# A hybrid long-convolution and attention step: the first modulation block issued from ScalarE's queue, and the filter network's first layer finished later

## The chip, the cores and the metric

The kernel runs on one core of a Trainium2 chip. The metric is the device time of one execution in microseconds; the kernel before is told by the median of three runs. The core's engines each run their own instructions in order: TensorE (PE in the profile; its weight loads are PEld), VectorE (DVE), ScalarE (ACT), GpSimd (POOL) and SyncE (SP), which issues most DMAs. ScalarE can issue DMAs too, on a queue of its own. An engine waits for another one, or for a DMA, on semaphores.

## The reference, cut to what matters

Two groups of tokens (128 prompt rows and 512 sample rows, 1024 channels each) go through one layer with shared weights. What the change touches is the beginning: a modulation made from a conditioning vector, the first projections of the modulated rows, and a small network that makes the filters of the long convolution.

```python
def modulation(cond, w_ada, b_ada):
    mod = jax.nn.silu(cond) @ w_ada + b_ada
    return jnp.split(mod, 3, axis=-1)

def hyena_filters(L, f_w1, f_b1, f_w2, f_b2, f_w3, f_freq):
    ...
    z = jnp.concatenate([t, jnp.cos(bands * w), -jnp.sin(bands * w)], axis=-1)
    hf = jnp.sin(f_freq[0] * (z @ f_w1 + f_b1))
    hf = jnp.sin(f_freq[1] * (hf @ f_w2 + f_b2))
    hf = (hf @ f_w3).astype(jnp.float32).reshape(L, 2, D_HYENA)
    ...

def layer_forward(x, cond, ctx_kv, p):
    shift, scale, gate = modulation(cond, p["w_ada"], p["b_ada"])
    h = x * (1 + scale) + shift
    (v_h, x1, x0, g_h), (q, k, v, g_a), m = split_projection(h, p["w_in"], p["conv_w"], p["conv_b"])
    ...                                   # filters, long convolution, attention
    out = merge_branches(y_h, g_h, y_a.reshape(g_a.shape), g_a, m, p["w_bh"], p["w_ba"], p["w_out"])
    x_new = layer_norm(ALPHA * x + gate * out, p["ln_g"], p["ln_b"])
    return x_new, kv_out
```

## The kernel before, in words

All 640 rows stand side by side as columns, and the 1024 channels are cut into eight blocks of 128 (`k` = 0 to 7). Every large product is made with operands split into a high and a low part (`hH` and `hL` for the modulated rows, `wh` and `wl`, or `wf` and `wg`, for weights) and three matmuls instead of one.

The change lies in `prologue()` (L267), which runs over the eight channel blocks. For each block:

- two loads of 512 KB bring the block's columns of `w_ada`, one for the shift (part 0) and one for the scale (part 1), into the two halves of a tile `ada{k}`; three buffers take turns (tags `X`, `dftL`, `F`). `ada()` (L257) issues the load and then the 16 small matmuls into `adaT` (`psa` in the code);
- one load of 512 KB (`xw`) brings the block's rows of x and the weights of three projections for that block; three buffers take turns (tag `raw`);
- ScalarE copies `adaT` to `row`, TensorE turns it into columns (`modT`, L341), VectorE adds the bias (`mod`, L346); then VectorE and ScalarE make `hx`, `hH`, `hL` and the split weights `wf`, `wg` (L328 to L357);
- TensorE adds the block's share to three projections (L177, 18 matmuls of 128x320 a block). This is done one block late: `script` says that the products of block 0 are made while the modulation of block 1 is worked out, and so on. Entries such as `"00"` and `"80 10"` are projections 0, 8 and 1 with block 0; entries such as `"w3"` are matmuls on zeros (L281) that compute nothing the output needs and only keep TensorE busy in block 0.

Beside this loop runs the filter network (`hidden_layers()`, L244, a generator). Each of its two layers (`sin_layer()`, L222) is a product on TensorE into `ps_f` (L228), eight short VectorE instructions that reduce the argument of a sine (L230 to L239, the first of them one for each half in the second layer), and a Sine on ScalarE (L241). `step(n)` runs the generator over `n` yields: `step(7)` at block 0 and then the pairs in `layers`, whose first number is run in the middle of a block and whose second one at its end. So `step` and `layers` decide where the network's instructions stand among those of the blocks. In the kernel before, the second layer's product follows at the end of block 0.

The order on each engine is that of the code, as far as a scheduler of the toolchain doesn't put independent instructions the other way round; DMAs issued through `load_to` (L63) keep their order on SP. Eight semaphores for DMAs take turns, so a ninth DMA waits for the landing of the first. At the start SP issues a small pack with the conditioning vectors (`pack0`, 17 KB), the filter network's inputs (`zemb`, 82.5 KB) and its weights (`pack1`, 98 KB), and then the loads of block 0. The pack is needed by ScalarE for the gate of the conditioning vector (L297) and so by the modulation's matmuls; the other two by the network's first product.

After the prologue come the long convolution, the attention and the merge, in which the projections (L177) and a grouped product (L1182) take most of TensorE's time. The change leaves the order of instructions on every engine as it was from block 5 on.

Of the kernel before, what the change touches and what calls it, by code (L numbers as in the profile page):

```python
# [9 lines left out]
F32 = mybir.dt.float32  # L10
# [36 lines left out]
def tile_hyena_natten_step(ctx: ExitStack, tc: tile.TileContext, a, o):  # L47
    nc = tc.nc
    P = 128

    def f(ap):
        return ap.bitcast(F32)
# [10 lines left out]
    def load_to(dst, src):  # L63
        ins = nc.sync.dma_start(dst, src)
        last[:] = [ins]
        if pinned[0]:
            tc.keep_in_program_order(ins)
# [33 lines left out]
    def aux(name):  # L101
        return ps_ax.tile([P, 512], F32, tag="aux", name=name)
# [9 lines left out]
    def row(pool, tag, name, dt=F32, bufs=NK + 1):  # L112
        return pool.tile([P, NT], dt, tag=tag, bufs=bufs, name=name)
# [5 lines left out]
    def load_pack(i):  # L119
        pack = const.tile([P, sum(n for _, n in PACKS[i])], F32, tag=f"pack{i}", name=f"pack{i}")  # L120
        load_to(pack[:], a[f"pack{i}"])
        c0 = 0
        for name, n in PACKS[i]:
            out[name] = pack[:, c0 : c0 + n]
            c0 += n
# [43 lines left out]
    def bank(i, ps_pair=None):  # L169
        return ps_pair or [acc(f"mm{i}_{hf}") for hf in range(2)]  # L170

    def accumulate(ps, w, k, xh, xl, lead=(0, 1, 2)):
        passes = (w[0], xh), (w[0], xl), (w[1], xh)
        for i in lead:
            wt, x = passes[i]
            for hf in range(2):
                nc.tensor.matmul(  # L177
                    ps[hf][:, :HALF], wt[k], x[:, hf * HALF : (hf + 1) * HALF],
                    start=(i == 0 and k == 0), stop=(i == lead[2] and k == NK - 1), skip_group_check=True,
                )  # L180
# [27 lines left out]
    hw = hy.enter_context(tc.tile_pool(name="hw", bufs=1, side="right"))  # L208
# [3 lines left out]
    def temp(tag, name, bufs=1):  # L212
        return hw.tile([P, NT], F32, tag=tag, bufs=bufs, name=name)
# [41 lines left out]
    nc.gpsimd.memset(st[:], 0.0)  # L255

    def ada(ch, ps, raw):  # L257
        load_to(raw, a["wada"][ch])
        for t in range(2):
            for j in range(4):  # L260
                kt = 4 * t + j
                nc.tensor.matmul(  # L262
                    ps[32 * j : 32 * j + 32, :], st[:, kt, :], raw[:, P * kt : P * kt + P],
                    start=(t == 0), stop=(t == 1), skip_group_check=True, tile_position=(0, 32 * j),
                )

    def prologue():  # L267
        script = (
            ("w3", "w1", "w3", "w4"), ("", "", "00", "80 10"), ("", "", "01", "81 11"), ("", "", "02", "82 12"),
            ("", "", "03", "83 13"), ("", "", "04", "84 14"), ("", "", "05", "85 15"), ("", "", "06", "86 16 07 87 17"),  # L270
        )
        layers = ((1, 1), (0, 2), (0, 2), (0, 2), (1, 1), (0, 0), (0, 0), (0, 0))
        nc.vector.memset(f(hid[:, :256]), 0.0)
        front = (0, 8, 1)
        parts = {}

        def work(items):
            for item in items.split():
                if item[0] == "w":
                    for _ in range(int(item[1:])):  # L280
                        nc.tensor.matmul(banks[0][0][:, :256], hid[:, :P], hid[:, :256], start=True, stop=True, skip_group_check=True)  # L281
                else:
                    i, j = int(item[0]), int(item[1])
                    c = P * front.index(i)
                    accumulate(banks[i], [{j: t[:, c : c + P]} for t in parts[j]], j, hH[:, j], hL[:, j], lead=(0, 2, 1))

        def step(n):
            for _ in range(n):
                next(filt, None)

        out["zemb"] = temp("u", "zemb", 4)[:33]
        load_to(out["zemb"], a["zemb"])
        load_pack(1)
        th0 = const.tile([P, 2 * NK], F32, tag="th0", name="th0")
        spare = const.tile([P, 1], F32, tag="spare", name="spare")
        nc.gpsimd.memset(spare[:], 0.0)
        nc.scalar.activation(th0[:], cc, AF.Tanh, scale=0.5)  # L297
        nc.scalar.activation(spare[:], spare[:], AF.Sin)
        nc.vector.scalar_tensor_tensor(th0[:], th0[:], 1.0, cc, op0=ALU.add, op1=ALU.mult)
        nc.vector.tensor_scalar_mul(st[:, :, 0:2], th0[:].rearrange("p (k c) -> p k c", c=2), 0.5)  # L300
        nc.vector.tensor_copy(bss[:, 0], out["bss"][:, :NK])
        nc.vector.tensor_scalar_add(bss[:, 1], out["bss"][:, NK:], 1.0)
        for i in front:
            banks[i] = bank(i, (aux("mm1lo"), aux("mm1hi")) if i == 1 else None)
        filt = hidden_layers()
        for k in range(NK):
            xw = wp.tile([P, 1024], F32, tag="raw", bufs=3, name=f"xw{k}")
            psa = aux(f"adaT{k}")
            if k == 0:
                work("w12")  # L310
                step(7)
            pool, tag = ((hw, "X"), (hyc, "dftL"), (hw, "F"))[k % 3]
            wt = pool.tile([P, 2048], F32, tag=tag, name=f"ada{k}")
            for part in range(2):
                work(script[k][part])
                ada(part * 8 + k, psa[:, part * P : part * P + P], wt[:, 1024 * part : 1024 * part + 1024])
            row_ = hwa.tile([P, 2 * P], F32, tag="fb", bufs=3, name=f"row{k}")
            nc.scalar.activation(row_[:], psa[:, : 2 * P], AF.Copy)
            load_to(xw[:], a["xw"][k])
            xt, wf = xw[:, :NT], xw[:, NT:]  # L320
            wh = row(yhp, "yh", f"wf{k}", F32R)[:, : 3 * P]
            wl = row(yhp, "yh", f"wg{k}", F32R)[:, : 3 * P]
            parts[k] = wh, wl
            step(layers[k][0])
            if k >= 6:
                split(wh, wl, wf)
            else:
                nc.scalar.activation(wh, wf, AF.Copy)  # L328
            if k == 7:
                wraw(9)  # L330
                load_pack(2)
                out["convw"] = out["convw"].rearrange("p (i c) -> p i c", c=4)
                wraw(2)
                load_filter(0)
                out["dft"] = hw.tile([P, 2560], F32, tag="F", name="draw")
                load_to(out["dft"][:, :1280], a["dft"][:, :1280])
                w9 = hw.tile([P, 2, 1024], F32R, tag="X", name="w9")
            psm = aux(f"modT{k}")
            work(script[k][2])
            for c in range(2):  # L340
                nc.tensor.matmul(  # L341
                    psm[:, c * 2 : c * 2 + 2], row_[:, c * P : c * P + P], sel,
                    start=True, stop=True, skip_group_check=True,
                )
            mod = const.tile([P, 2, 2], F32, tag="mod", bufs=4, name=f"mod{k}")
            nc.vector.tensor_tensor(  # L346
                mod[:], psm[:, 0:4].rearrange("p (s c) -> p s c", s=2),
                bss[:, :, k : k + 1].to_broadcast([P, 2, 2]), op=ALU.add,
            )
            hx = hwa.tile([P, NT], F32, tag="cv", bufs=2, name=f"hx{k}")  # L350
            for c, s0, n in ((0, PC, LP), (1, SC, LS)):
                cs = slice(s0, s0 + n)
                nc.vector.tensor_scalar(hx[:, cs], xt[:, cs], mod[:, 1, c : c + 1], mod[:, 0, c : c + 1], op0=ALU.mult, op1=ALU.add)
                nc.scalar.activation(hH[:, k, cs], xt[:, cs], AF.Identity, scale=mod[:, 1, c : c + 1], bias=mod[:, 0, c : c + 1])
            if k < 6:
                nc.vector.tensor_tensor(wl, wf, f(wh), op=ALU.subtract)
            nc.vector.tensor_tensor(hL[:, k], hx[:], f(hH[:, k]), op=ALU.subtract)  # L357
            if k == 7:
                raw = raws.pop(9)
                nc.scalar.activation(w9[:, 0], raw[:], AF.Copy)  # L360
                low = nc.vector.tensor_tensor(w9[:, 1], raw[:], f(w9[:, 0]), op=ALU.subtract)
                early[2] = wtile(2)
                early[9] = [[w9[:, i, c : c + P] for c in range(0, 1024, P)] for i in range(2)]
            work(script[k][3])
            step(layers[k][1])
        now(filt)
        last.append(low)
# [1343 lines left out]
```

## Time and profile before

| | |
|---|---|
| median of 3 runs | 863.28 us (860.81 to 864.22) |
| profiled execution | 860.83 us, span 859.1 us |
| PE busy | 849.4 us, 99% of the span |
| DVE, ACT, POOL busy | 678.7, 464.7, 131.4 us |
| DMA | 138.64 MB, mean 161 GB/s |
| DMA in the first 43 us (two slices of 40) | 352 and 359 GB/s |

The profile is a record of one execution. Its span runs from the first to the last instruction; the execution's own time is 1.7 us longer. In a timeline row the first number is the start in us after the span's start, the second the time from the start of the row's first instruction to the end of its last, then come engine, line of the kernel, operation, written and read tiles, size and count; what stands in brackets is the engine's idle time before the row and what ended it. "PEld" rows are weight loads, "SPq" rows the issuing of a DMA by SP.

### The profile page before, as it was taken

The page shows a single profiled execution, that of the slowest core. Times are in us where ns is not written, and L with a number is a line of the kernel's source. Part 1 is how long each engine was busy: PE and PEld are TensorE (multiplying, and loading weights), DVE is VectorE, ACT ScalarE, POOL GpSimd, SP SyncE. Part 2 cuts the span into 40 slices and gives each one's busy share as a digit, 9 for nine tenths or more (in the row PEclk, how much of TensorE's full clock was granted, in tenths as well). Part 3 has the DMA queues.
Part 4 walks back from the last instruction along what each step waited for, and adds up shares of the span by engine and source line. Part 5 has one row for each costly group of instructions (what it writes and reads, how often), then busy time and mean ns, then how long its engine had stood idle before and what let it go on. Part 6 is the DMA issues. An engine that isn't in the chain of part 4 may idle for free.

```text
span 859.1 us, 16817 instructions
## 1 busy us (share of the span) xinstructions
PE 849.4 (99%) x6387; PEld 822.7 (96%) x6387; DVE 678.7 (79%) x1408; ACT 464.7 (54%) x996; POOL 131.4 (15%) x140
## 2 busy tenths in 40 slices
PE   9999999999999999999999999999999999999996
PEld 7999999999999999999999999999999999999885
DVE  6777695697759559789988897889888778799776
ACT  4675656545554643646665676666655654345310
POOL 0010010101001010105232225124222200000000
PEclk9999999999999999999999999999999999999999
DMA  9986575656657558774263535354354386445621
GB/s 352 359 256 144 109 149 126 153 122 144 127 134 150 126 146 187 168 251 148 85 195 90 192 95 189 106 177 149 105 173 118 111 266 202 173 131 140 246 107 54
DMA packets 56868, 138.64 MB, mean 161 GB/s; under 512 B 8495, under 2 KB 23859, under 8 KB 56788
## 3 DMA queue, kind: packets, MB, share of 16 engines
q1 hardware_dynamic: 45412, 111.69, 39.7%
q0 software_dynamic: 5760, 20.19, 14.4%
q10 hardware_dynamic: 5616, 5.70, 1.9%
q8 instruction: 50, 0.82, 0.4%
q14 instruction: 30, 0.25, 0.1%
HBM read 121.43 MB, written 16.12 MB: 160 GB/s over the span
## 4 chain that ended last, share of the span: by engine, by line
PE 95%; DMA 3%; DVE 1%; SPq 0%; ACT 0%; issue 0%; DVEq 0%
PE sp L1182 33%; PE mm L177 30%; PE out L1534 6%; PE v L917 5%; PE pt L1019 3%; PE s L1026 3%; PE s L979 2%; PE mm L191 2%; PE ve L929 1%; DMA raw<-wall 1%; DMA wl<-wall 1%; DMA ada<-wada 1%; PE adaT L262 1%; PE yb L166 1%; PE yb L165 1%; PE yb L167 1%
## 5 line engine op out<-in xcount | busy, mean ns | idle before, releaser
L1182 PE MATMUL sp<-t,wb 128*128 128x320 f32 x912 | 141.7, 310 | 0.0
L1182 PEld LDWEIGHTS sp<-t,wb 128*128 128x128 f32 x912 | 134.9, 188 | 0.9 <-ACT pp L1047 0.5
L1182 PE MATMUL sp<-hH,wb 128*128 128x320 f32 x456 | 111.2, 314 | 0.0
L177 PE MATMUL mm<-hH,wl 128*128 128x320 f32 x448 | 105.5, 309 | 0.1
L177 PE MATMUL mm<-hH,wh 128*128 128x320 f32 x448 | 104.9, 309 | 0.0
L177 PE MATMUL mm<-hL,wh 128*128 128x320 f32 x448 | 104.2, 310 | 0.0
L157 POOL DMA_DIRECT2D wl<-wall x37 | 32.2, 870 | 329.5 <-ACT wl L156 263.3
L108 ACT ACTIVATE wb<-s 128x512 fp32r<-128x512 f32 x92 | 56.3, 627 | 45.6 <-DVE s L1142 26.6
L1182 PEld LDWEIGHTS sp<-hH,wb 128*128 128x128 f32 x456 | 78.4, 188 | 2.3 <-issue 2.1
L158 ACT ACTIVATE wh<-raw 128x1024 fp32r<-128x1024 f32 x37 | 39.2, 1059 | 70.8 <-PE mm L177 65.3
L177 PEld LDWEIGHTS mm<-hH,wl 128*128 128x128 f32 x448 | 75.5, 188 | 0.9 <-DMA wl<-wall 0.4
L177 PEld LDWEIGHTS mm<-hH,wh 128*128 128x128 f32 x448 | 75.2, 188 | 0.5
L177 PEld LDWEIGHTS mm<-hL,wh 128*128 128x128 f32 x448 | 75.1, 188 | 0.3
L109 DVE TENSOR_TENSOR wb<-s,wb 128x512 fp32r<-128x512 f32 x92 | 62.5, 692 | 10.3 <-ACT wb L108 10.3
L1182 PE MATMUL sp<-hL,wb 128*128 128x320 f32 x228 | 70.4, 309 | 0.0
L108 ACT ACTIVATE wb<-raw 128x512 fp32r<-128x512 f32 x66 | 41.4, 628 | 44.4 <-PE sp L1182 23.5
L1001 POOL TENSOR_SCALAR p<-p,sm 128x384 f32<-128x384 f32 x32 | 44.5, 1399 | 102.7 <-DVE sm L1000 102.7
L109 DVE TENSOR_TENSOR wb<-raw,wb 128x512 fp32r<-128x512 f32 x66 | 46.6, 705 | 5.5 <-ACT wb L108 5.4
L177 PE MATMUL mm<-yhs,wh 128*128 128x320 f32 x256 | 47.9, 309 | 0.0
L1197 DVE TENSOR_TENSOR c<-sp,u 128x320 f32<-128x320 f32 x69 | 33.5, 486 | 12.0 <-PE sp L1182 12.0
L1182 PEld LDWEIGHTS sp<-hL,wb 128*128 128x128 f32 x228 | 42.8, 188 | 0.0
L1001 POOL TENSOR_SCALAR edge<-edge,sm 128x320 f32<-128x320 f32 x32 | 41.9, 1318 | 0.5 <-DVE sm L1000 0.5
(385 smaller groups left out, 2078.3 us busy)
## 6 DMA issues: line engine op xcount, KB each, us to landing
raw<-wall SPq DMA_DIRECT2D x93, 512.0 KB, 3.6
wl<-wall POOLq DMA_DIRECT2D x37, 512.0 KB, 5.8
ada<-wada SPq DMA_DIRECT2D x16, 512.0 KB, 9.2
tm<-bias SPq DMA_DIRECT2D x16, 512.0 KB, 4.5
xw<-xw SPq DMA_DIRECT2D x8, 512.0 KB, 9.4
gate<-wgate SPq DMA_DIRECT2D x8, 512.0 KB, 4.1
wo<-wall SPq DMA_DIRECT2D x8, 512.0 KB, 5.3
dec<-decay SPq DMA_DIRECT2D x20, 128.0 KB, 3.0
```

Of the source, the lines that this page charges most:

```text
L108: hi = nc.scalar.activation(dst_h, src, AF.Copy)
L109: return hi, (eng or nc.vector).tensor_tensor(dst_l, src, f(dst_h), op=ALU.subtract)
L157: nc.gpsimd.dma_start(wl, a["wall"][i], accum_op=ALU.add)
L158: nc.scalar.activation(wh, raw[:], AF.Copy)
L177: nc.tensor.matmul(ps[hf][:, :HALF], wt[k], x[:, hf * HALF : (hf + 1) * HALF], start=(i == 0 and k == 0), stop=(i == lead[2] and k == NK - ...
L917: nc.tensor.matmul(ps[t // 2][:, t % 2 * 256 : t % 2 * 256 + 256], x[:, k, P * t : P * t + P], wk, start=first and t % 2 == 0, stop=last, ...
L1001: nc.gpsimd.tensor_scalar_mul(pv, pv, sm[:, 2:3])
L1019: nc.tensor.transpose(pt[:, i * P : i * P + P], x, ident)
L1026: nc.tensor.matmul(dst, lhs, rhs, start=start, stop=stop, skip_group_check=True)
L1182: nc.tensor.matmul(dst, wk, x(xi, k), start=j < 4 and k == 0 and i == 0, stop=k == 3 and i == 2, skip_group_check=True,)
L1197: after = nc.vector.tensor_tensor(c, dst, c if j == 3 else u, op=ALU.add)
L1534: ins = nc.tensor.matmul(dst, m[k][:, c0 : c0 + P], w[:, c : c + n], start=(first and k == 0), stop=(last and k == 5), skip_group_check=True,)
```

## The change

The load of part 0 of block 0 (`ch` = 0) is taken out of `ada()`. It is issued in the prologue's first lines, from ScalarE's queue, and stands there ahead of every other instruction of ScalarE, the loading of its function tables too. SP's three small loads stand where they stood; behind them SP issues part 1 of block 0 where part 0 stood, and everything after it one place sooner.

The filter network's generator is run over five yields at block 0 instead of seven, and `layers` is changed to match. The last two VectorE instructions of the first layer go behind the rows of block 0, the first layer's Sine goes to the middle of block 1, and the second layer's product to the end of block 1. The second layer's further instructions follow by some places each, and its Sine, in the middle of block 4 before, stands at the end of block 4.

```diff
     def ada(ch, ps, raw):
-        load_to(raw, a["wada"][ch])
+        if ch:
+            load_to(raw, a["wada"][ch])
...
-        layers = ((1, 1), (0, 2), (0, 2), (0, 2), (1, 1), (0, 0), (0, 0), (0, 0))
+        layers = ((0, 2), (1, 2), (0, 2), (0, 2), (1, 2), (0, 0), (0, 0), (0, 0))
...
+        first = hw.tile([P, 2048], F32, tag="X", name="ada0")
+        tc.keep_in_program_order(nc.scalar.dma_start(first[:, :1024], a["wada"][0]))
         out["zemb"] = temp("u", "zemb", 4)[:33]
         load_to(out["zemb"], a["zemb"])
         load_pack(1)
...
                 work("w12")
-                step(7)
+                step(5)
             pool, tag = ((hw, "X"), (hyc, "dftL"), (hw, "F"))[k % 3]
-            wt = pool.tile([P, 2048], F32, tag=tag, name=f"ada{k}")
+            wt = pool.tile([P, 2048], F32, tag=tag, name=f"ada{k}") if k else first
```

On SP, at the program's start: `pack` is a small load, `zemb` the network's input, `ada` a half of a modulation block, `xw` a block's rows. Before:

```order
L64 DMA pack_84<-pack 128x34
L64 DMA zemb<-zemb 33x640
L64 DMA pack_123<-pack 128x196
L64 DMA ada_165<-wada 128x1024 x2
L64 DMA xw_140<-xw 128x1024
```

Now:

```order
L64 DMA pack_84<-pack 128x34
L64 DMA zemb<-zemb 33x640
L64 DMA pack_125<-pack 128x196
L64 DMA ada_121<-wada 128x1024
L64 DMA xw_142<-xw 128x1024
```

One of the two loads of block 0 is gone from SP; it stands first on ScalarE (L293 of the changed kernel).

On TensorE, at the end of block 0 and the beginning of block 1, before: `modT` is the modulation of block 0, `mm<-hid` the matmuls on zeros, `ps_f<-hf` the filter network's second product, `adaT` the modulation matmuls of block 1, `mm<-hH` the first projection products of block 0.

```order
L341 MATMUL modT_195<-pack_84,row_188 128x2 x2
L281 MATMUL mm_0_134<-hid 128x256 x4
L228 MATMUL ps_f_214<-hf_154,pack_123 128x320
L228 MATMUL ps_f_215<-hf_154,pack_123 128x320
L262 MATMUL adaT_221<-ada_222,st 32x128 x16
L177 MATMUL mm_0_134<-hH,wf_191 128x320
```

Now, at the same place and then at the end of block 1, ahead of the modulation matmuls of block 2:

```order
L344 MATMUL modT_192<-pack_84,row_186 128x2 x2
L282 MATMUL mm_0_136<-hid 128x256 x4
L263 MATMUL adaT_214<-ada_215,st 32x128 x16
L177 MATMUL mm_0_136<-hH,wf_189 128x320
...
L177 MATMUL mm1lo<-hL,wf_189 128x320
L177 MATMUL mm1hi<-hL,wf_189 128x320
L228 MATMUL ps_f_271<-hf_156,pack_125 128x320
L228 MATMUL ps_f_272<-hf_156,pack_125 128x320
L263 MATMUL adaT_279<-ada_280,st 32x128 x16
```

The two matmuls of the network's second layer have moved from ahead of block 1's modulation to behind the projection products of block 0.

## The prediction

> **What bounds the kernel now.** I read first the page's busy times and its chain, then the chain of waits of the first 16 us, then TensorE's timeline there, then the windows with DMA rates.
>
> ```profile
> span 859.1 us, 16817 instructions
> PE 849.4 (99%) x6387; PEld 822.7 (96%) x6387; DVE 678.7 (79%) x1408; ACT 464.7 (54%) x996; POOL 131.4 (15%) x140
> PE 95%; DMA 3%; DVE 1%; SPq 0%; ACT 0%; issue 0%; DVEq 0%
> ```
>
> TensorE bounds the kernel: it is busy for 849.4 of 859.1 us, and the chain is made of it to 95%. All of its idle time is 9.7 us, so a change of the first 16 us can give only what TensorE waits there, and can take what TensorE is given to do. The chain of that stretch:
>
> ```profile
> 2.02 0.43 SPq L64
> ...
> 3.92 7.09 DMA ada<-wada
> 11.00 0.04 issue
> 11.05 0.65 PE adaT L262 x16
> ...
> 14.97 1.01 PE adaT L262 x32
> ```
>
> The chain runs through SP's issues, then through the DMAs of the modulation blocks until 11.00, and from 11.05 on through TensorE alone. So the place that decides is the landing of block 1's second half at 11.00: what lands sooner counts until there, and what TensorE does after it counts in full. Its timeline:
>
> ```profile
> 1.17 2.93 PE L281 MATMUL mm<-hid 128*128 128x256 f32 x12 [1.17 <-DVE hid L273]
> ...
> 4.03 1.18 PE L228 MATMUL ps_f<-zemb,pack 33*64 33x320 f32 x4
> 5.14 0.62 PE L281 MATMUL mm<-hid 128*128 128x256 f32 x3
> ...
> 6.07 0.65 PE L262 MATMUL adaT<-ada,st 128*32 128x128 f32 x16 [0.31 <-DMA ada<-wada]
> 6.64 0.38 PE L281 MATMUL mm<-hid 128*128 128x256 f32 x1
> 7.27 0.64 PE L262 MATMUL adaT<-ada,st 128*32 128x128 f32 x16 [0.24 <-DMA ada<-wada]
> ...
> 8.88 0.72 PE L281 MATMUL mm<-hid 128*128 128x256 f32 x4
> 9.54 0.81 PE L228 MATMUL ps_f<-hf,pack 64*128 64x320 f32 x4
> 10.28 1.42 PE L262 MATMUL adaT<-ada,st 128*32 128x128 f32 x32
> 11.62 0.56 PE L177 MATMUL mm<-hH,wf 128*128 128x320 f32 x2
> ```
>
> TensorE waits for block 0's halves (0.31 and 0.24 us), fills with matmuls on zeros, does the filter network's second product (9.54) while block 1 is still on its way, and gets to the first useful projection product at 11.62. The windows:
>
> ```profile
> core 0: us, PE busy (x) PEld busy (x) DVE busy (x) ACT busy (x) POOL busy (x), PEclk, DMA share, GB/s
> 1.00:2.00 1.00, 0.83 (x4) 0.83 (x5) 0.12 (x1) 1.00 (x1) 0.40 (x12) 1.00 0.10 11
> 2.00:3.00 1.00, 1.00 (x6) 1.00 (x6) 0.17 (x1) 0.44 (x3) 0.00 (x0) 1.00 0.62 147
> 3.00:4.00 1.00, 1.00 (x6) 0.80 (x4) 0.32 (x3) 1.00 (x1) 0.00 (x0) 1.00 0.87 164
> 4.00:5.00 1.00, 1.00 (x5) 0.29 (x4) 0.00 (x0) 0.26 (x2) 0.00 (x0) 1.00 0.98 385
> 5.00:12.00 7.00, 6.32 (x87) 4.22 (x86) 5.93 (x14) 2.60 (x6) 0.00 (x0) 1.00 1.03 418
> 12.00:16.00 4.00, 4.00 (x55) 3.61 (x53) 3.23 (x8) 1.87 (x4) 0.00 (x0) 1.00 1.02 412
> ```
>
> From 5 to 12 the DMA engines are full at 418 GB/s and TensorE idles 7.00 - 6.32 = 0.68 us. From 12 on TensorE has no idle time. A block's half (524,288 bytes) takes 524288 / 418000 = 1.25 us of the full stream.
>
> **Part 1: the first half goes out sooner.** The queues at the start:
>
> ```profile
> 0.73 0.38 SPq L64 DMA_DIRECT2D pack<-pack  x1
> 1.63 0.35 SPq L64 DMA_DIRECT2D pack<-pack  x1
> 2.02 0.90 SPq L64 DMA_DIRECT2D ada<-wada  x2
> ...
> 0.72 1.28 ACT L297 ACT_TABLE_LOAD   x1 [0.72 <-PEq L1699]
> 2.54 0.22 ACT L297 ACTIVATE th<-pack 128x16 f32<-128x16 f32 x1 [0.54 <-DMA pack<-pack]
> ```
>
> ScalarE is free at 0.72, so block 0's first half goes out 1.3 us sooner than at 2.02. Its second half takes the place at 2.02, and all that follows on SP is issued about 0.45 us sooner, half of the 0.90 us of the two issues; since the stream is full, the landing counts, not the issue. ScalarE pays for the issue: some 0.4 us, as an issue of SP costs, ahead of a table load of 1.28 us, which then ends at 2.4 instead of 2.0. The wait of 0.54 us for the small pack covers that (2.54). Without this cover the gate would come 0.4 us later, and nobody waits for it before 5.8.
>
> What the stream gains has two bounds. By the bytes of the three windows from 2 to 5 (147 + 164 + 385 = 696 KB of 3 x 418 = 1254 KB), 558 KB had room: the whole half fits, and everything behind it lands 1.25 us sooner. By the busy share of the same windows (0.62, 0.87, 0.98) only 0.53 us were free. [...] Block 1's second half then lands at 11.00 - 1.1 = 9.9.
>
> When could TensorE use it? Taking out the two waits, the rows from 6.07 on start up to 0.55 us sooner; the four matmuls on zeros at 8.88 then end at 9.60 - 0.55 = 9.05, and with the network's product gone from there, block 1's first half is worked at 9.0 instead of 10.28 and the second half could be at 9.0 + 0.65 = 9.65. That is before 9.9, so the DMA still decides, and 11.05 becomes 9.95: 1.1 us gained at this place. The modulation of block 0 keeps up if VectorE does:
>
> ```profile
> 7.68 0.49 DVE L237 SCALAR_TENSOR_TENSOR E<-E 128x320 f32<-128x320 f32 x1
> 8.21 0.33 DVE L239 TENSOR_SCALAR E<-E 128x320 f32<-128x320 f32 x1
> 9.06 0.16 DVE L346 TENSOR_TENSOR mod<-modT,bss 128x4 f32<-128x4 f32 x1 [0.53 <-PE modT L341]
> ...
> 10.57 0.83 DVE L357 TENSOR_TENSOR hL<-hx,hH 128x640 fp32r<-128x640 f32 x1
> ```
>
> With the two instructions at 7.68 and 8.21 gone behind the row block, VectorE is free at 7.65, `mod` can be made 0.55 us sooner, at 8.5, and `hL` ends at 11.40 - 0.55 = 10.85. The product of block 0 now begins near 10.5 and reads `hL` only with its third pair of matmuls, some 0.7 us later. That fits with 0.35 us to spare.
>
> **Part 2: the network's second product on TensorE.** Before, it stood from 9.54 to 10.28, 0.74 us, in time in which TensorE would have waited for block 1 anyway. Now it stands behind the products of block 0, in the window from 12 to 16 where TensorE is busy for 4.00 of 4.00 us. There the 0.74 us count in full. So much of the gain is paid back: the filter's work is not removed, it loses its cover.
>
> The rest of the moved pieces costs nothing: VectorE is busy for 3.23 of 4 us in the window from 12 on, ScalarE for 1.87, and the later place of a Sine (0.47 us) and of two VectorE instructions (0.49 + 0.33) stays within that. The changed order on SP at block 4 (a small load behind `xw` instead of ahead of it) lies in a full stream.
>
> **Sum.** -1.1 + 0.74 = -0.36 us at 12 us, and TensorE's dense row carries it on. With the stream gaining 0.53 us it is +0.21; with 1.25 it is -0.51. For the profiled execution: 860.83 - 0.36 = 860.5 us. That execution lies at the low end of the three runs (860.81 to 864.22, median 863.28). The mean of these four executions is 862.3, and I set the forecast from it: 862.3 - 0.36, rounded to **861.9 us**. The runs scatter by more than the effect; less than 0.5% (4.3 us) can hardly be told from no change.
>
> **The rivals.**
>
> *The small loads are held up, and it gets slower.* The first half shares the 16 DMA engines with the pack and the network's two inputs. The row that bears on it:
>
> ```profile
> pack<-pack SPq DMA_DIRECT2D x1, 98.0 KB, 2.0
> ```
>
> Issued at 1.63, the weights land at about 3.6, and the network's product starts at 4.03 behind the matmuls on zeros: 0.4 us of slack. If every engine finishes its share of the big half first, the weights come up to 1.25 us later, the product starts at 4.9, and the chain through TensorE, ready at 9.65, is ready at 9.65 + 0.85 = 10.5. Then 11.05 becomes 10.5, and with the 0.74 us of part 2 the kernel is 0.2 us slower. It gets worse if TensorE's rate suffers: a product of the same kind took 1.18 us at 4.03 and 0.81 at 9.54, so TensorE is slow at first and the 4.2 us of rows between 5.14 and 9.60 could take up to 1.18 / 0.81 as long if the pause delays that: 2.0 us more, +2.2 us in all, 864.5. The point from which it decides is a delay of the weights by more than 0.7 us (0.4 of slack and the 0.3 from 9.65 to 9.95). [...] As to the rate, the windows show a granted clock of 1.00 throughout, so only the lengths show the slow beginning. [...]
>
> *The gain gets lost later.* The chain after the prologue:
>
> ```profile
> 36.06 0.33 SPq L64
> 36.39 0.04 issue
> 36.43 4.27 DMA w<-fw
> ...
> 40.78 8.92 DMA raw<-wall
> ```
>
> Here DMAs are on the chain. If they didn't start sooner with the prologue, the gain would end there: no change, 862.3. Against it: the issue at 36.06 directly follows ScalarE's work on block 6, which moves with TensorE.
>
> *The product costs nothing at its new place* because the rows of block 1 make TensorE wait there. Then the whole 1.1 us stays: 861.2. Against it stands the window from 12 to 16 without idle time.
>
> **How the numbers follow.** The forecast gets 0.62, the held-up loads 0.20, the lost gain 0.12, the free product 0.06. None of them reaches 4.3 us by its own price; what is left for that are effects of the shift on the other 840 us that no row shows, to which I give 0.03 for faster and 0.05 for slower, so 0.92 for within 0.5%. The range takes the fastest and the slowest run shown as the scatter of a median: 860.81 less 0.51, so 860.3, to 864.22 with the held-up loads' smaller price, 0.2, and half a microsecond of their larger one: 864.9.
>
> **What would show it.** Right: the first `adaT` row follows the matmuls on zeros without a wait for a DMA; block 1's second half is worked near 9.95; `ps_f<-hf` stands near 13.8 to 14.5; block 2's `adaT` starts near 14.5 instead of 14.9. Wrong: `ps_f<-zemb` starts well after 4.03 with a wait for a DMA, or `adaT` of block 1 waits beyond 10.5; or the distance to the old timeline at 60 us is not the one at 16 us; or the median lies outside 860.3 to 864.9.

## The result, and the profile after

The kernel with the change takes 865.43 us (median of 10 executions, 863.31 to 866.42); the kernel before, beside it on the same chip, takes 863.31 us (median of 10, 860.45 to 864.88). The ratio is 1.0031, with a 95% interval of 1.0017 to 1.0045: slower, by less than 0.5%, where the prediction had 861.9 us and a small gain. The median lies above the predicted range.

The profiled execution (863.31 us) is the shortest of the ten. The page's head of it:

```profile
span 861.5 us, 16816 instructions
PE 849.2 (99%) x6387; PEld 822.8 (95%) x6387; DVE 678.0 (79%) x1408; ACT 465.1 (54%) x996; POOL 131.5 (15%) x140
```

TensorE does the same work as before (849.2 against 849.4 us), so the 2.4 us of span are idle time. Its timeline at the beginning shows where they lie:

```profile
5.40 0.76 PE L228 MATMUL ps_f<-zemb,pack 33*64 33x320 f32 x4 [1.29 <-DMA pack<-pack]
...
6.63 0.64 PE L263 MATMUL adaT<-ada,st 128*32 128x128 f32 x16
...
7.60 0.64 PE L263 MATMUL adaT<-ada,st 128*32 128x128 f32 x16
...
10.11 0.64 PE L263 MATMUL adaT<-ada,st 128*32 128x128 f32 x16 [0.17 <-DMA ada<-wada]
11.37 0.65 PE L263 MATMUL adaT<-ada,st 128*32 128x128 f32 x16 [0.62 <-DMA ada<-wada]
11.94 0.56 PE L177 MATMUL mm<-hH,wf 128*128 128x320 f32 x2
...
15.22 0.81 PE L228 MATMUL ps_f<-hf,pack 64*128 64x320 f32 x4
16.73 1.08 PE L263 MATMUL adaT<-ada,st 128*32 128x128 f32 x32 [0.70 <-DVE E L230]
```

Three things stand there that were not listed in the old timeline: a wait of 1.29 us for the pack of weights ahead of the network's first product, waits of 0.17 and 0.62 us for the two halves of block 1, and, behind the network's second product, a wait of 0.70 us for VectorE. And two that were there before are gone: both halves of block 0 are worked without a wait. That is no gain, though: TensorE gets to them later than before (6.63 and 7.60 instead of 6.07 and 7.27). Set beside the old rows:

| place on TensorE | before | after | later by |
|---|---|---|---|
| network's first product starts | 4.03 | 5.40 | 1.37 |
| first projection product (L177) | 11.62 | 11.94 | 0.32 |
| end of block 0's products: what stands next | 14.90 | 15.22 | 0.32 |
| `adaT` of block 2 | 14.90 | 16.73 | 1.83 |
| grouped product, just before its late load | 791.18 | 792.78 | 1.60 |
| grouped product, with that load | 791.32 | 793.72 | 2.40 |
| end of the span | 859.1 | 861.5 | 2.4 |

The step from 1.60 to 2.40 us is a weight load that lands late in this execution. First the two rows of the timeline after, then the two of before:

```profile
792.78 0.31 PE L1185 MATMUL sp<-ya_hL,wb 128*128 128x320 f32 x1
793.72 0.56 PE L1185 MATMUL sp<-ya_hH,wb 128*128 128x320 f32 x2 [0.63 <-DMA wb<-wall]
```

```profile
791.18 0.31 PE L1182 MATMUL sp<-ya_hL,wb 128*128 128x320 f32 x1
791.32 0.46 PE L1182 MATMUL sp<-ya_hH,wb 128*128 128x320 f32 x2
```

In another execution of the changed kernel (e6 below) this wait was 0.30 us, and e2 has none there but one of 1.00 us for a weight load at 61 us; such waits vary by execution and are no fixed price of the change.

The chain of waits of the first 17 us now has three parts: the DMA of block 1's second half until 11.32, TensorE, and a short piece of VectorE.

```profile
3.45 7.87 DMA ada<-wada
...
11.37 0.65 PE adaT L263 x16
...
15.29 0.79 PE ps_f L228 x4
16.08 0.60 DVE E L230
...
16.73 0.30 PE adaT L263
```

The windows, with the DMA engines' busy share and GB/s in the last two columns:

```profile
2.00:3.00 1.00, 1.00 (x6) 1.00 (x6) 0.00 (x0) 0.45 (x1) 0.00 (x0) 1.00 0.70 205
3.00:4.00 1.00, 1.00 (x6) 0.81 (x4) 0.00 (x0) 0.13 (x1) 0.00 (x0) 1.00 1.01 393
4.00:5.00 1.00, 0.10 (x1) 0.00 (x0) 0.50 (x4) 0.98 (x2) 0.00 (x0) 1.00 1.03 269
5.00:12.00 7.00, 5.81 (x84) 3.79 (x84) 4.82 (x11) 2.69 (x6) 0.00 (x0) 1.00 1.01 390
```

From 2 to 5 us the stream moved 205 + 393 + 269 = 867 KB, 171 KB more than before; from 5 to 12 it ran at 390 instead of 418 GB/s, 196 KB less. Most of the lead goes within one microsecond, and by 8 us it is used up. The window in which it goes, after and then before:

```profile
5.00:6.00 1.00, 0.60 (x4) 0.22 (x4) 0.00 (x0) 0.59 (x2) 0.00 (x0) 1.00 0.92 303
```

```profile
5.00:6.00 1.00, 0.76 (x5) 0.41 (x3) 0.71 (x2) 0.00 (x0) 0.00 (x0) 1.00 1.01 410
```

The packets in the two traces (one for each row of a load) show what happened. In the changed kernel the half's 128 packets pass from 1.83 to 4.14 us, and the packets of the network's two small loads from 3.59 to 4.76; before, these two passed from 2.14 to 3.26. So the half goes ahead of the small loads. Behind them the stream of large loads starts slowly: its packets of 4 KB take 0.29 us on average from 4 to 5 us and 0.20 from 5 to 6, against 0.16 from 8 us on. Before, there was one such slow start, from 3 to 4 us (0.40), and from 4 us on they took 0.16 to 0.17. The slow packets from 4 to 6 us are there in e1, e3, e5, e6 and e12 below too, all with the half ahead, and in none of the other traces of the old loads (e2, e7, e9, e10); from 5 to 8 us the stream moved 358, 340, 355 and 352 GB/s in the changed kernel, e1, e5 and e6, and 414, 400, 400 and 407 in the kernel before, e7, e9 and e10. Why the packets are slow there is not shown. Nor do the bytes explain all of the delay: they are level from 8 us on, and block 1's second half still lands 0.32 us later, at 11.32 instead of 11.00.

The tables of DMA issues of the first 6 us (KB each, us from issue to landing) have the half in ScalarE's queue and the smallest pack, first after, then the pack before:

```profile
ada<-wada ACTq DMA_DIRECT2D x1, 512.0 KB, 4.0
...
pack<-pack SPq DMA_DIRECT2D x1, 17.0 KB, 3.1
```

```profile
pack<-pack SPq DMA_DIRECT2D x1, 17.0 KB, 1.8
```

The 17 KB, issued at the same 0.73 as the half, take 3.1 instead of 1.8 us, and ScalarE's Tanh starts with them at 3.87 instead of 2.54:

```profile
0.73 0.41 ACTq L293 DMA_DIRECT2D ada<-wada  x1
1.17 1.28 ACT L300 ACT_TABLE_LOAD   x1 [1.17 <-PEq L1702]
3.87 0.22 ACT L300 ACTIVATE th<-pack 128x16 f32<-128x16 f32 x1 [1.42 <-DMA pack<-pack]
```

### The profile page after: what moved, and what is told of

Same layout as the page of the kernel before. It is cut to its first block, busy times and chain, and to the rows that moved or that the text cites. A ratio compares the mean times of both kernels' runs of the same rounds, so it can differ in the third digit from the quotient of the medians.

```text
span 861.5 us, 16816 instructions
## 1 busy us (share of the span) xinstructions
PE 849.2 (99%) x6387; PEld 822.8 (95%) x6387; DVE 678.0 (79%) x1408; ACT 465.1 (54%) x996; POOL 131.5 (15%) x140
## 3 DMA queue, kind: packets, MB, share of 16 engines
HBM read 121.43 MB, written 16.12 MB: 160 GB/s over the span
## 4 chain that ended last, share of the span: by engine, by line
PE 96%; DMA 2%; issue 1%; DVE 1%; SPq 0%; ACT 0%; DVEq 0%; POOLq 0%
PE mm L177 32%; PE sp L1185 31%; PE out L1537 6%; PE v L920 5%; PE pt L1022 3%; PE s L1029 3%; PE s L982 2%; PE mm L191 2%; PE ve L932 1%; DMA ada<-wada 1%; DMA wb<-wall 1%; PE adaT L263 1%; PE yb L166 1%; PE yb L165 1%; PE yb L167 1%
## 5 line engine op out<-in xcount | busy, mean ns | idle before, releaser
L177 PE MATMUL mm<-hH,wl 128*128 128x320 f32 x448 | 105.5, 309 | 0.0
L177 PE MATMUL mm<-hH,wh 128*128 128x320 f32 x448 | 105.0, 309 | 0.0
L177 PE MATMUL mm<-hL,wh 128*128 128x320 f32 x448 | 104.2, 310 | 0.0
L177 PEld LDWEIGHTS mm<-hH,wl 128*128 128x128 f32 x448 | 75.5, 188 | 0.8 <-DMA wl<-wall 0.2
L177 PEld LDWEIGHTS mm<-hH,wh 128*128 128x128 f32 x448 | 75.2, 188 | 0.5
L177 PEld LDWEIGHTS mm<-hL,wh 128*128 128x128 f32 x448 | 75.1, 188 | 0.3
L109 DVE TENSOR_TENSOR wb<-s,wb 128x512 fp32r<-128x512 f32 x92 | 62.1, 687 | 10.1 <-ACT wb L108 10.1
L177 PE MATMUL mm<-yhs,wh 128*128 128x320 f32 x256 | 47.9, 309 | 0.0
```

The costliest lines, as they stand in the source:

```text
L109: return hi, (eng or nc.vector).tensor_tensor(dst_l, src, f(dst_h), op=ALU.subtract)
L177: nc.tensor.matmul(ps[hf][:, :HALF], wt[k], x[:, hf * HALF : (hf + 1) * HALF], start=(i == 0 and k == 0), stop=(i == lead[2] and k == NK - ...
```

## The experiments

Every run is compared with the kernel before on the same chip in the same batch; the median of before was 861.5 to 861.6 us in all three batches. Differences "on average" are those of the means of 10 to 12 executions from those of 33 to 35 of the kernel before; the brackets behind them are 95% intervals.

**The two parts of the change, each alone.** e1 keeps the issue on ScalarE and puts the filter network's instructions back; e2 keeps the new order and puts the load back on SP.

```diff
 # e1, from the changed kernel
-        layers = ((0, 2), (1, 2), (0, 2), (0, 2), (1, 2), (0, 0), (0, 0), (0, 0))
+        layers = ((1, 1), (0, 2), (0, 2), (0, 2), (1, 1), (0, 0), (0, 0), (0, 0))
-                step(5)
+                step(7)
```

> Only the issue from ScalarE; the filter network's order as before. Theory A (three separate prices: small loads held up by the big one on the same DMA engines, about 0.3 us at 12 us; the network's second product without cover, 0.74 us; a wait of block 2's modulation matmuls until VectorE has read that product out of its bank, 0.77 us): the network's first product starts near 5.4 instead of 4.03, block 1's second half is worked near 11.4 instead of 11.05, and TensorE stays 0.3 to 0.5 us behind the kernel before from 12 us on. Theory B (the loss all comes from the disturbed loads, the product is free at its new place): TensorE is 1.8 us behind at 30 us. By the prediction's sum it would be 1.1 us ahead.

Measured: 862.68 us, ratio 1.0010 [0.9995, 1.0025], on average +0.74 us [-0.3, 1.8]. TensorE's timeline:

```profile
5.36 0.76 PE L228 MATMUL ps_f<-zemb,pack 33*64 33x320 f32 x4 [1.26 <-DMA pack<-pack]
...
10.75 1.39 PE L263 MATMUL adaT<-ada,st 128*32 128x128 f32 x32
12.08 0.55 PE L177 MATMUL mm<-hH,wf 128*128 128x320 f32 x2
...
15.34 1.08 PE L263 MATMUL adaT<-ada,st 128*32 128x128 f32 x32
```

The wait for the weights is there in full (1.26), the gain is not: the first projection product stands at 12.08 against 11.62, and block 2 at 15.34 against 14.90, 0.44 us late, without any wait for VectorE. So in its trace the earlier issue alone costs about 0.45 us of TensorE's path instead of giving 1.1 (the total time does not show it by itself, its interval includes zero), and the wait of 0.70 us belongs to the other part.

```diff
 # e2, from the kernel before
-        layers = ((1, 1), (0, 2), (0, 2), (0, 2), (1, 1), (0, 0), (0, 0), (0, 0))
+        layers = ((0, 2), (1, 2), (0, 2), (0, 2), (1, 2), (0, 0), (0, 0), (0, 0))
-                step(7)
+                step(5)
```

> Only the filter network's order as in the change; all loads on SP as before. Theory A: nothing until 14.9 us, then 0.74 us for the product and 0.77 us for the wait on VectorE's reading, so TensorE 1.5 us behind at 30 us and later. Theory B: no change at 30 us. A third theory for the wait (VectorE is behind with block 1's rows because the loads were late): the wait gets shorter by what the loads come sooner here, 0.3 us, so 1.2 us behind.

Measured: 863.42 us, ratio 1.0015 [1.0003, 1.0028], on average +1.24 us [0.4, 2.0]. TensorE's timeline:

```profile
4.03 1.22 PE L228 MATMUL ps_f<-zemb,pack 33*64 33x320 f32 x4
...
11.72 0.56 PE L177 MATMUL mm<-hH,wf 128*128 128x320 f32 x2
...
14.99 0.81 PE L228 MATMUL ps_f<-hf,pack 64*128 64x320 f32 x4
16.50 1.08 PE L262 MATMUL adaT<-ada,st 128*32 128x128 f32 x32 [0.70 <-DVE E L230]
```

Here all loads are on time (4.03), and until block 2 the kernel is within 0.1 us of the one before (14.99 against 14.90). Then come the product and the same wait of 0.70 us: 16.50 against 14.90, which is 0.09 for the start, 0.74 for the product and 0.77 for the wait. VectorE is not late: the chain above shows it beginning to read the first half of `ps_f` (L230) just as the product ends, and needing 0.60 us for it.

The two parts together, 0.74 + 1.24 = 1.98 us, agree with the whole change: +2.30 us [1.1, 3.5] in the first comparison.

**Why TensorE waits for VectorE behind the product.** The accumulators come from a pool of four banks (`aux`), which `adaT`, `modT`, both halves of `ps_f`, and for projection 1 `mm1lo` and `mm1hi` share. At the end of block 0, where the product stood, the latter two had not been written. At the end of block 1 they hold two of the four banks, the two halves of `ps_f` take the others, and block 2's `adaT` has to wait until VectorE has read one of them. e3 makes and reads one half at the end of block 1 and the other at the end of block 2, so that one bank stays free.

```diff
 # e3, from the changed kernel (sin_layer, L225)
-        ps = [aux(f"ps_f{n}{i}") for i in range(n // 320)]
-        for i, r0, w, x in products:
...
-        yield
+        for j in range(n // 320):
+            p = aux(f"ps_f{n}{j}")
+            for i, r0, w, x in products:
+                if i == j:
...
+            yield
-        layers = ((0, 2), (1, 2), (0, 2), (0, 2), (1, 2), (0, 0), (0, 0), (0, 0))
+        layers = ((0, 2), (1, 1), (0, 2), (0, 2), (0, 3), (1, 1), (0, 0), (0, 0))
```

> The change as it is, but the network's second product in two halves, one at the end of block 1 and one at the end of block 2, each in one accumulator bank, and VectorE reads each half on its own. Theory A (with only two free banks both halves together leave none for block 2's modulation matmuls): no wait of the modulation matmuls for VectorE, TensorE 1.1 to 1.3 us behind the kernel before at 30 us instead of 1.8. If VectorE's lateness made the wait and not the banks: the wait stays, 1.8 us behind at 30 us.

Measured: 864.40 us, ratio 1.0025 [1.0012, 1.0038], on average +2.32 us [1.6, 3.0]. TensorE's timeline:

```profile
17.60 0.80 PE L230 MATMUL ps_f<-hf,pack 64*128 64x320 f32 x2
18.33 1.08 PE L264 MATMUL adaT<-ada,st 128*32 128x128 f32 x32
...
22.62 0.80 PE L230 MATMUL ps_f<-hf,pack 64*128 64x320 f32 x2
23.35 1.08 PE L264 MATMUL adaT<-ada,st 128*32 128x128 f32 x32
```

No wait for VectorE is left, as the theory of the banks has it. But each half takes 18.33 - 17.60 = 0.73 us, as long as both together in the changed kernel (0.74): 1.46 us in all against 0.74 + 0.77. So nothing is won, and the expected gain (1.1 to 1.3 us behind instead of 1.8) did not come. The timeline as a whole is later than the changed kernel's (17.60 against 15.22) for another reason, which the next runs are about: in this execution TensorE ran slowly from 8 to 15 us, and its first product waited 1.79 us for the weights.

**The rate of TensorE in the first 17 us.** e6 is the changed kernel once more, e10 the kernel before once more, both without an edit. e5, e7 and e9 change only the number of matmuls on zeros at the start: e5 fills the pause of the changed kernel, e7 makes a pause in the kernel before, e9 lengthens the filling of the kernel before.

```diff
 # e5, from the changed kernel
-                work("w12")
+                work("w18")
 # e7, from the kernel before
-                work("w12")
+                work("w6")
 # e9, from the kernel before
-                work("w12")
+                work("w15")
```

> The change once more, to compare within one job and to have a second trace of it. Theory A: 1.5 us behind the kernel before at block 2 from the product and the wait for its bank, and 0.3 us or more from the loads; where the trace shows half rate within the first 16 us, 1 to 2 us more. Rival: the same times at every place as in the first trace, and the scatter comes from late DMAs near 60 and 790 us only.

> The kernel before against itself: no difference within the interval; how far two equal kernels lie apart tells what the other comparisons can bear. If its trace is of the slower group, theory A expects half rate beyond 5 us in it and TensorE 1 to 3 us behind the first trace by 16 us; the rival expects late DMAs near 60 or 790 us instead.

Measured: e6 864.39 us, ratio 1.0029 [1.0016, 1.0042], on average +2.35 us [1.3, 3.4], as in the first comparison. e10 861.72 us, ratio 0.9999 [0.9984, 1.0015]. The traces of both differ from the first ones of the same kernels. TensorE's timeline of e6, and its window from 8 to 14 us (granted clock in the third column from the end):

```profile
5.72 0.76 PE L228 MATMUL ps_f<-zemb,pack 33*64 33x320 f32 x4 [1.63 <-DMA pack<-pack]
...
8.22 1.08 PE L263 MATMUL adaT<-ada,st 128*32 128x128 f32 x16 [0.30 <-DMA ada<-wada]
...
13.75 0.90 PE L177 MATMUL mm<-hH,wf 128*128 128x320 f32 x2
...
18.99 1.08 PE L263 MATMUL adaT<-ada,st 128*32 128x128 f32 x32 [0.70 <-DVE E L230]
```

```profile
8.00:14.00 6.00, 5.78 (x60) 4.67 (x61) 3.82 (x9) 2.11 (x5) 0.00 (x0) 0.50 1.02 417
```

and the timeline of e10, the kernel before, with its window:

```profile
6.23 1.08 PE L262 MATMUL adaT<-ada,st 128*32 128x128 f32 x16
...
12.79 1.75 PE L262 MATMUL adaT<-ada,st 128*32 128x128 f32 x32
14.47 0.56 PE L177 MATMUL mm<-hH,wf 128*128 128x320 f32 x2
```

```profile
8.00:14.00 6.00, 6.00 (x55) 4.43 (x51) 3.98 (x9) 2.35 (x5) 0.00 (x0) 1.00 1.02 417
```

The 16 modulation matmuls take 0.64 us at the full rate and 1.08 in these rows. In e6 TensorE starts at the full rate and has half of it from about 8 to 14.5 us (0.50 in the window); in e10 it comes to the full rate only near 14 us, and the first projection product stands at 14.47 instead of 11.62. So both kernels have executions in which the first 15 us cost up to 3 us more, about as much as the executions of one kernel differ (860.36 to 864.67 in e10). All 14 traces bear this out: `adaT` of block 2 starts anywhere from 14.68 to 20.18 us, and from there to the end of the span it is 843.7 to 845.8 us in every one. What these executions differ by is thus mostly made in the first 20 us. The wait for VectorE is 0.70 us in e6 and e5 too.

> The change with six more matmuls on zeros ahead of the network's first product (18 instead of 12), so that TensorE has work while the small loads are late. Theory A (part of the loss comes from TensorE's clock: the pause of 1.3 us makes some executions start slow or fall back to half rate): the path of an undisturbed execution is the same as the change's, 1.6 to 1.8 us behind the kernel before at 30 us, but the executions scatter less and the mean is 0.5 to 1.5 us below the change's in the same job. Rival (the clock has no part in it): mean and scatter as the change's.

> The kernel before with six matmuls on zeros less (6 instead of 12): TensorE pauses from about 2.8 to 4.0 us and starts the network's first product at the same time as before, so no path is longer. Theory A: more executions start or fall back to half rate, the mean is 0.5 to 2 us above the kernel before. Rival (the clock has no part): no difference beyond 0.3 us.

> The kernel before with three matmuls on zeros more (15 instead of 12): TensorE starts the network's first product about 0.6 us later but is busy without gaps for longer. [...] Rival (the clock has no part): +0.0 to +0.3 us in every execution.

Measured: e5 863.11 us, ratio 1.0018 [1.0004, 1.0031], on average 0.94 us less than e6 beside it, with an interval of -2.2 to +0.3 that does not exclude zero. e7 863.29 us, ratio 1.0019 [1.0007, 1.0031], on average +1.06 us [0.1, 2.0]. e9 862.12 us, ratio 0.9997 [0.9984, 1.0010]. e7 computes just what the kernel before does. In its trace the network's first product waits 0.88 us for the weights and starts at 3.70, TensorE is at half rate until 8.5 us, and the first projection product stands only 0.34 us later than before (11.96). The rest of the +1.06 us would have to come from executions that the trace does not show; but the interval reaches down to 0.1, so that a pause ahead of the network's first product makes the slow beginnings more frequent is suggested and not shown. Filling the pause (e5) does not settle it either, since its own trace was at half rate too, without a pause:

```profile
5.31 1.33 PE L228 MATMUL ps_f<-zemb,pack 33*64 33x320 f32 x4
...
7.51 1.08 PE L263 MATMUL adaT<-ada,st 128*32 128x128 f32 x16
```

What decides in one execution when the full rate comes stays open; the last section has the times.

**What holds up the small loads.** e4 gives ScalarE the network's two small loads and lets SP begin with block 0 behind the smallest pack. e8 lets ScalarE issue only a quarter of the half (256 of 1024 columns) and SP the rest at the old place. e11 lets ScalarE issue the half behind its Tanh. e12 gives everything to SP, with the half first. All four have the old order of the network.

```diff
 # e4
-        load_to(out["zemb"], a["zemb"])
-        load_pack(1)
+        load_to(out["zemb"], a["zemb"], nc.scalar)
+        load_pack(1, nc.scalar)
 # e8
+        tc.keep_in_program_order(nc.scalar.dma_start(first[:, :256], a["wada"][0][:, :256]))
 # e11
         tc.keep_in_program_order(nc.scalar.activation(th0[:], cc, AF.Tanh, scale=0.5))
+        tc.keep_in_program_order(nc.scalar.dma_start(first[:, :1024], a["wada"][0]))
 # e12
+        load_to(first[:, :1024], a["wada"][0])
+        load_pack(0)
         ...
         load_to(out["zemb"], a["zemb"])
```

> The filter network's order as before; ScalarE issues the network's input and weights as its first instructions, SP issues the small pack and then the modulation blocks at once. Theory A (whoever has its packets in the queues first delays the other, and a small load pays more): the gate's Tanh starts near 2.9 instead of 2.54, the network's first product between 4.0 and 5.0, block 1's second half 0.3 to 0.9 us before 11.05, so TensorE up to 0.5 us ahead at 30 us. If the big loads always win against small ones of another queue: the product starts after 5.2 and TensorE is behind.

> Filter order as in the kernel before; ScalarE issues only a quarter of the first half (256 of 1024 columns, 128 KB), SP the other three quarters where the half stood. Theory A (small loads are late by what the big one has in the queues): the Tanh starts near 2.9 instead of 3.87 with the whole half, the network's first product at 4.0 to 4.5, block 1's second half 0.2 to 0.4 us before 11.05; TensorE 0 to 0.4 us ahead of the kernel before at 30 us. Rival (any second queue costs the small loads the same, whatever its size): the product near 5.4 and TensorE 0.3 us or more behind, as with the whole half.

> Filter order as in the kernel before; ScalarE issues the first half only after its Tanh, near 2.8 us, when the small pack has landed and the other small loads are in the queues. Theory A (a small load is late only if a big one is in another queue's turn ahead of it): the network's first product starts at 4.0 to 4.2 as in the kernel before, and TensorE is within 0.4 us of it at 16 us. Rival (any big load on ScalarE's queue delays SP's small ones): the product after 4.8.

> Filter order as in the kernel before; all on SP, but the first half is issued ahead of the three small loads, with nothing on ScalarE. Theory A (small loads wait for a big one that gets its turn first, in one queue or in two): the Tanh starts near 3.8 to 4.2 and the network's first product at 4.6 to 5.6, TensorE 0.2 to 1 us behind at 16 us. Rival (two queues at once are what costs): in one queue the small loads follow at once, the product at 4.0 to 4.5 and TensorE level with the kernel before or ahead.

Measured: e4 863.72 us, ratio 1.0016 [1.0002, 1.0030]. e8 863.32, 1.0017 [1.0005, 1.0029]. e11 865.94, 1.0043 [1.0027, 1.0058]. e12 864.69, 1.0023 [1.0008, 1.0038]. The rows that tell them apart, from TensorE's timelines of e4, e8, e11 and e12 in this order:

```profile
5.36 1.33 PE L228 MATMUL ps_f<-zemb,pack 33*64 33x320 f32 x4 [1.25 <-DMA pack<-pack]
```

```profile
5.62 1.33 PE L228 MATMUL ps_f<-zemb,pack 33*64 33x320 f32 x4 [1.52 <-DMA pack<-pack]
```

```profile
4.03 1.33 PE L228 MATMUL ps_f<-zemb,pack 33*64 33x320 f32 x4
...
7.65 1.08 PE L263 MATMUL adaT<-ada,st 128*32 128x128 f32 x16 [1.35 <-DMA ada<-wada]
```

```profile
5.98 1.33 PE L226 MATMUL ps_f<-zemb,pack 33*64 33x320 f32 x4 [1.88 <-DMA pack<-pack]
```

With everything in SP's one queue (e12) the weights are late too, so it does not take a second queue to hold them up; the order of the loads is enough. That they are later still there (5.98) is not shown to be the order's doing: seven of their 128 packets took 0.3 to 1.3 us each in this execution, against 0.04 us for such a packet in the traces of the kernel before and the changed one. With ScalarE's half behind the small loads (e11) the weights are on time at 4.03, and now it is the half that comes late (1.35 us of waiting): its first packet starts at 5.02, when 99 of the 128 packets of the half that SP had issued 0.35 us earlier are through. In e4 the small loads lose though it is they that sit in ScalarE's queue: the weights, issued at 1.39 behind SP's first half of 1.17, pass from 3.90 to 4.84. So in these traces what is issued first is served first, and with a half issued ahead of them, in the same queue or in the other one, the small loads let the network's product start 1.3 to 2.0 us later.

Several expectations failed. In e4 the product starts after 5.2, as the rival to its theory had it. In e12 both the Tanh (4.46) and the product (5.98) are later than expected. In e8 a quarter of the bytes on ScalarE did not shorten the delay, 5.62 against 5.36 in e1. Its packets show an accident of that execution: 124 of the weights' 128 packets had passed by 3.53 us (all of them by 3.26 before), and one of 784 bytes took from 3.42 to 5.03, with three behind it. So e8 does not decide between its theory and its rival.

All four of these traces came to TensorE's full rate only near 16 or 17 us, so their later rows are to be set beside e10, which was slow to start as well. There the first projection product stands at 14.47; in e4, e8, e11 and e12 it stands at 15.97, 16.12, 16.07 and 16.59, which is 1.50 to 2.12 us later. In these four TensorE does not wait for block 1 at all, and what the first late load costs (1.33, 1.59 and 1.95 us at `ps_f` in e4, e8 and e12, 1.42 at block 0's half in e11) passes through in full; what is above it, at most 0.2 us, is the later full rate (block 1's 32 modulation matmuls take 1.82 to 1.94 us instead of 1.75). In the changed kernel and in e1, at the full rate, 1.37 and 1.33 us of delay at `ps_f` become 0.32 and 0.46, because there TensorE has to wait for block 1 anyway. e11 is the slowest of all, 3.87 us [3.1, 4.6] above the kernel before on average; how much of that is the rate is not shown.

No run beats the kernel before; e9 and e10 are level with it, and e1 cannot be told from it.

## Why the prediction was wrong, by its own steps

- *The first half goes out sooner: -1.1 us.* This step failed. The half was issued at 0.73, and the next four loads of SP about 0.45 us sooner, as predicted (block 1's `xw`, the ninth load, had to wait for the half's landing, 4.0 us after its issue, and went out at 4.77 instead of 4.43). But block 1's second half is worked at 11.37 instead of 9.95, and TensorE's path is 0.32 us later (0.45 in e1). The 1.1 us stands near the bound by bytes (558 KB of room, 1.25 us) and far from the one by busy shares (0.53 us), and no run shows it. What the trace of before shows is that the weights' 784-byte packets took 0.04 us each, and that where the share was high and the rate low, from 3 to 4 us, it was the first large packets that took 0.40 instead of 0.16 us. What the changed kernel gained is the lead in bytes at 5 us, 171 KB, worth 0.41 us at 418 GB/s, close to the bound by busy shares; it was lost again by 8 us, when the stream of large loads started slowly behind the small ones. Why it did, and what made the landing 0.32 us later, stays open. That it belongs to the early issue is shown: the first projection product stands at 11.94 with it and 11.72 without in the network's new order (changed kernel and e2), and at 12.08 and 11.62 in the old one (e1 and the kernel before).
- *The rival "the small loads are held up".* Its chance was 0.20, and its first half is what happened: the half goes ahead of the small loads, and `ps_f` waits for the pack (5.40 against the 4.9 that it worked out). Its step from there to the time is another matter. It had TensorE's own chain decide, ready for block 1's second half at 10.5. That chain was ready at 10.58 (the first half's row at 10.11 less its wait of 0.17, and 0.64 for its matmuls), and then TensorE waited for the load until 11.37: as before, the landing decided, and it came later still. So the sign was right, and the path to it was not, except for executions that begin at half rate, where the late weights do pass through in full.
- *The network's product without its cover: +0.74.* Right. From the product's start to block 2's `adaT` 1.51 us pass, in the changed kernel and in e2, 0.70 of them idle; the product's own row is 0.81, and the 0.07 more is its overlap with the next matmul, lost through the wait.
- *"The rest of the moved pieces costs nothing."* Wrong, and the largest term of the loss. The step looked at whether VectorE had time (3.23 of 4 us) and not at who must wait for its result. At its new place the product takes the last two of four accumulator banks, and TensorE waits for VectorE's read: 0.77 us in the changed kernel, and the same wait in e2, e5 and e6; none in e1 and e3.
- *ScalarE's issue is covered; VectorE keeps up with the modulation.* Right: the table load ends 0.45 us later, the pack later still, and the first projection product follows the modulation without a wait for VectorE.
- *Sum.* -0.36 became 0.32 + 0.74 + 0.77 = +1.83 us at block 2, and TensorE's dense row did carry it on: 1.60 us are left at 792 us. So the rival "the gain gets lost later" had no gain to lose, and the "free product" falls with the 0.74.
- *TensorE's rate.* The rival's second half (a pause that delays the full rate, up to +2.2 us) is partly borne out: e6 and e3, with pauses of 1.63 and 1.79 us, lost the full rate at 8 us, and in e6 the first projection product stands 1.8 us behind the first trace (13.75 against 11.94). That the kernel before has slow beginnings without any pause (e10) was not seen, and their share in the +2.3 us is not settled.
- *The forecast's base.* It was the mean of the four executions, 862.3; over ten the mean is 863.0. That is 0.7 of the 3.5 us between 861.9 and the median of 865.43; the remaining 2.8 are the change, +2.3 instead of -0.36 by the means, and 0.1 between mean and median.

## What to carry to other kernels

A transfer that is brought forward does not simply fill room: in these runs it went ahead of the loads issued behind it, in its own queue and in the other one. So first ask who waits for the loads that it overtakes, and put small loads with waiting readers ahead of large ones. Work that is moved on TensorE takes its accumulator banks along: count at the new place how many buffers of the pool are held, and if it takes the last one, add the time until another engine has read it (0.77 us here). Busy time on the reading engine said nothing about that wait: VectorE was busy for 3.23 of the 4 us from 12 to 16 in the kernel before, and for 2.59 with the change. And what a late load costs depends on what TensorE would wait for next: a delay of 1.3 us cost 0.3 to 0.5 us where another load was the later one, and all of it where none was.

## What the runs showed of the hardware that was not expected

The rate of TensorE at the start differs between executions of one and the same program. 16 modulation matmuls took 0.64 or 1.08 us by it, and the traces' records of the granted clock say when the full rate begins:

| full rate from (us) | traces |
|---|---|
| 4.4 to 5.0 | the kernel before, the changed kernel, e1, e2, e9 |
| 4.5 and 4.8, lost at 7.9 and 8.2, again from 14.8 and 15.0 | e6, e3 |
| 8.5, 10.1, 14.2 | e7, e5, e10 |
| 15.9 to 17.3 | e4, e8, e11, e12 |

In the traces of the table's first row matmuls run from 1.17 us, and the full rate comes 3.3 to 3.8 us later. In e5 and e10 TensorE had its matmuls on zeros from 1.17 us on too, then the network's product without a wait, and still came to the full rate only at 10.1 and 14.2. In e6 and e3 the full rate was lost 3.4 us after it had come, and for 6.8 us; TensorE was idle for 1.2 us of those 3.4 in both. The changed kernel and e1, idle for 0.8 and 0.9 us of the 3.4 behind their own beginning, kept the full rate. These are four traces, and whether idle time is what counts was not tested. The profile's column of the granted clock reads 1.00 in e10's window from 8 to 14 us although the lengths there are those of half the rate, because its records begin only with the full rate; so at the start the lengths are the better witness.
